# A two-layer decoder trunk: the transposes of two residues' probabilities together, and split weights in six half-tile buffers

## The chip, the cores and the metric

The kernel runs on one core of a Trainium2 chip. The metric is the time of one execution on the device in microseconds (us), lower is better. A core has five engines with a queue each, worked through in order: PE (TensorE, matrix products; its weight loads are shown as PEld), DVE (VectorE), ACT (ScalarE), POOL (GpSimd) and SP (SyncE, which here issues the DMAs). They meet through semaphores.

## What is computed

Two decoder layers over 256 tokens of width 1024, in float32. Layer 0 mixes tokens with three groups of dilated causal window attention, 16 heads each; layer 1 with gated linear attention (GLA). Each is followed by a convolutional gated channel mixer. Cut from the reference:

```python
for i in range(DEPTH):
    mod = jax.nn.silu(c) @ w_ada[i] + b_ada[i]
    sh1, sc1, g1, sh2, sc2, g2 = jnp.split(mod, 6, axis=-1)
    h = rmsnorm(x, norm_mix[i]) * (1.0 + sc1) + sh1
    y = dilated_mixture(h, ...) if i == 0 else gla_mixer(h, ...)
    x = x + g1 * y
    h = rmsnorm(x, norm_ffn[i]) * (1.0 + sc2) + sh2
    x = x + g2 * conv_ffn(h, ...)
return rmsnorm(x, norm_final)
```

In the attention, `p = softmax(q k^T + bias)` over a window, `o = p v` for each of the three groups, and the three outputs are mixed by the softmax of their log sums.

## The kernel before, in words

Activations lie transposed, 8 tiles `x[kt]` of 128 features by 256 tokens. All large products are done three times: an operand is split into a high part in the reduced format `float32r` and the remainder, and `mm3` (L172, matmuls at L175, L176, L177) adds high times high, high times low and low times high.

**Weights.** `split` (L155) loads a tile of up to 2048 columns through SP into one of four `raw` buffers, casts each half on ACT into a `whi` tile (L165), and writes the remainder of each half on DVE into a `wlo` tile (L169). `whi` and `wlo` come from the pool `wspl` (L65), three buffers each of 2048 columns. Matmuls may start on a half as soon as that half is written; a buffer comes free when all matmuls that read any part of its tile are done, and a raw buffer when both subtractions are done. `parts` (L326) hands out columns of the two tiles.

**Stages.** First the norm, while adaLN weights (`ada_chunk`, L129) and the tiles `w0[kt]` (15 blocks of 128 columns: q and k of units 0 and 1, v of unit 0) are loaded. Then eight attention units, `u` = 0 to 7, a pair of heads in all three groups each: products of q, k (`pqk`) and v (`pv`), then `attend` (L408). Then `project` (L569): four tiles `w_out_a[n]`, `n` = 0 to 3, each with columns for kt 0 to 7 in order, 256 each, and `o[kt]` is the output of unit kt. Behind each `n` stand two residuals (L322, tile `py` into `x`), their squares (L199), scaled copies `early_x` (L287) and sums of squares (`sqacc`, L202). `ffn` (L603) then splits the second half of the first `w_up` tile and the second `w_up` tile (the latter held behind `sixth`, the scaled copy of kt 5 and a sum, L605), and `rstd_of` (L184) turns the sums into the norm with two matmuls `ms` (L187). The last residual, kt 7, is held behind the sum before it (L321). Then 22 pairs of up products (`pab`) and the down products (`pd`). Layer 1 has GLA in place of attention, with gates `pr` (`gate`, L887).

**Attention.** In `attend` the queries of a unit are taken as four residues `r` (token index modulo 4), in two halves `h`. For each residue, scores `s` (L419, L426) get their bias and maximum on DVE (L437), exponentials on ACT (L446), and are normed on DVE into `pn` (two instructions, L452 and L453; three `pn` buffers). Three transposes on PE (L457) bring them into a `t` bank, which ACT (even `r`) or DVE (odd `r`) copies to `pt` (L458). The products `po` (L462, L466) follow, and `ohi` on ACT and `olo` on DVE (L471, L472) split the unit's output.

**What sets the order.** The program is written in the order of the source, and a planner in the framework puts each engine's instructions in an order of its own: it simulates the engines, takes at each point what is ready with the earliest place in the source, and gives out a pool's buffers when its model says that one is free. `behind` and `issue_after` hold an instruction behind others in that order. On the chip each engine then keeps to its order, whatever really is ready. So a change of buffers can change the order everywhere.

Of the kernel before, what the change touches and what calls it, by code (L numbers as in the profile page):

```python
# [11 lines left out]
F32 = mybir.dt.float32  # L12
# [6 lines left out]
P = 128  # L19
# [38 lines left out]
def trunk(ctx: ExitStack, tc: tile.TileContext, I, out):  # L58
# [6 lines left out]
    wspl = ctx.enter_context(tc.tile_pool(name="wspl", bufs=3))  # L65
# [17 lines left out]
    c_row = wspl.tile([P, 2048], F32, tag="whi", name="c_row")  # L83
# [12 lines left out]
    oh = wspl.tile([P, 2048], F32, tag="whi", name="oh")  # L96
# [55 lines left out]

    last_load, copied, last_lo = [None], [None], [None]

    def split(src, n, dmas=1, after=((), ()), late=(), low=()):  # L155
        raw = wraw.tile([P, 2048], F32, tag="raw", name="raw")
        for i in range(dmas):
            c = slice(n * i // dmas, n * (i + 1) // dmas)
            last_load[0] = nc.sync.dma_start(raw[:, c], src[:, c])
        hi = wspl.tile([P, 2048], F32R, tag="whi", name="whi")  # L160
        lo = wspl.tile([P, 2048], F32R, tag="wlo", name="wlo")
        for i in range(0, n, n // 2):
            c = slice(i, i + n // 2)
            with behind(*after[i > 0]):
                copied[0] = nc.scalar.copy(hi[:, c], raw[:, c])  # L165
        for i in range(0, n, n // 2):
            c = slice(i, i + n // 2)
            with behind(*(late if i else low)):
                last_lo[0] = nc.vector.tensor_tensor(lo[:, c], raw[:, c], hi[:, c].bitcast(F32), op=ALU.subtract)  # L169
        return hi, lo  # L170
# [155 lines left out]
    def parts(w, at, n=P):  # L326
        return w[0][:, at : at + n], w[1][:, at : at + n]
# [23 lines left out]
    sq = wspl.tile([P, 2048], F32, tag="wlo", name="sq").rearrange("p (k t) -> p k t", k=KT)  # L351
    with behind(last_c):
        keep_warm(4)
    nc.vector.tensor_tensor(sq[:, 0:4, :], x_all[:, 0:4, :], x_all[:, 0:4, :], op=ALU.mult)
    with behind(silu):
        for i in (4, 6):
            last_sq = nc.scalar.activation(sq[:, i : i + 2, :], x_all[:, i : i + 2, :], AF.Square)
    for n in (0, 4):
        for m in (2, 1):
            last_add = nc.vector.tensor_tensor(sq[:, n : n + m, :], sq[:, n : n + m, :], sq[:, n + m : n + 2 * m, :], op=ALU.add)  # L360
# [4 lines left out]
    r = rstd_of([sq[:, 0, :], sq[:, 4, :]])  # L365
# [12 lines left out]
    for kt in range(KT):  # L378
        with behind(*first):
            term = ada_chunk(0, kt, dmas=1 if kt else 2)  # L380
        h.append(normed(0, 0, r, kt))
        if kt:
            w0.append(split(I["w0"][kt], 15 * P))
        else:
            with behind(chain[0][1]):
                w0.append(split(I["w0"][kt], 15 * P, 2, after=((term,), (chain[0][0],))))
# [21 lines left out]
    def attend(u, q, k, v, bias):  # L408
# [32 lines left out]
        for h in range(2):  # L441
            rs = slice(2 * h, 2 * h + 2)
            nc.vector.tensor_scalar(m[:, 4:8][:, rs], m[:, 0:4][:, rs], -1.0, None, op0=ALU.mult)
            for r in (2 * h, 2 * h + 1):
                c = prob[r][:, 0 : KEYS + r]
                nc.scalar.activation(c, c, AF.Exp, bias=m[:, 4 + r : 5 + r], accum_out=m[:, 8 + r : 9 + r])  # L446
            nc.vector.reciprocal(m[:, 12:16][:, rs], m[:, 8:12][:, rs])
            for r in (2 * h, 2 * h + 1):

                f = m[:, 12 + r : 13 + r]  # L450
                pn = att.tile([P, KEYS], F32, tag="pn", name="pn", bufs=3)
                nc.vector.tensor_scalar(grouped(pn[:, 0:T]), by_residue(prob[r][:, 0:T]), f, None, op0=ALU.mult)  # L452
                nc.vector.tensor_scalar(pn[:, T:KEYS], prob[r][:, T + r : KEYS + r], f, None, op0=ALU.mult)  # L453
                t = bank("t", "t")
                for j in range(3):
                    c = slice(P * j, P * j + P)
                    last_t[0] = nc.tensor.transpose(t[:, c], pn[:, c], ident)  # L457
                (nc.vector.tensor_copy if r % 2 else nc.scalar.copy)(pt[:, r, :], t[:, 0:KEYS])  # L458
# [50 lines left out]
    for u in range(NPAIR):  # L509
# [10 lines left out]
        if u == 0:  # L520
# [5 lines left out]
            for kt in range(KT):  # L526
# [3 lines left out]
                wv = parts(w0[kt], 6 * P, NG * P)  # L530
# [3 lines left out]
                for i in range(2 * NG):  # L534
                    mm3(pqk1[i], parts(w0[kt], 9 * P + P * i), h[kt], s and i % 2 == 0, e and i % 2 == 1)
# [67 lines left out]
    def ffn(l, early):  # L603
# [4 lines left out]
        with tc.tile_pool(name=f"ffn{l}", bufs=2) as pool:  # L608
# [57 lines left out]
            for f2 in range(0, KT, 2):  # L666
# [3 lines left out]
                for half, f in ((0, 0), (0, 1), (1, 0), (1, 1)):  # L670
                    w = split(I["w_down"][l, f2 + f, half], 11 * P)
# [300 lines left out]
    y = wspl.tile([P, 2048], F32, tag="whi", name="y")  # L972
    for half in range(2):
        for t, own in enumerate(halves):
            c = slice(512 * half, 512 * half + 512)
            d = y[:, D * t : D * t + D][:, c]
# [29 lines left out]
def _laid_out(a):  # L1006
# [3 lines left out]
    def vec(v):  # L1010
# [76 lines left out]
```

## Time and profile before

| what | value |
|---|---|
| median of three runs | 789.2 us (789.19 to 790.78) |
| profiled execution | 786.27 us, of which its span 784.5 us |
| granted PE clock, mean | 0.996 |
| DVE busy, ACT busy, of the span | 644.3 us, 481.8 us |
| casts L165, subtractions L169 | 274 each, 245.7 and 291.8 us |
| transposes L457 | 96, in groups of three |
| DMA traffic | 184.72 MB, 235 GB/s |

The span goes from the first to the last instruction of the profiled execution; the execution's own time has 1.8 us more around it. In rows of the trace's timeline the first number is the start in us, the second how long the group of instructions took, then engine, line, operation, the tiles (written<-read), shapes and count; brackets at the end hold the idle time of the engine before it and what ended it. In the view of waits a row reads: who waited, for whom, us in total, times, longest.

### The profile page before, as it was taken

What the parts mean: (1) busy time and instruction counts of PE and PEld (TensorE: products, weight loads), DVE (VectorE), ACT (ScalarE), POOL (GpSimd) and SP (SyncE); (2) the same over time, 40 slices, a digit from 0 to 9 for tenths busy, and PEclk for the clock granted to TensorE, in tenths of its full rate; (3) what the DMA queues carried; (4) which work ended last, traced back from release to release, by engine and by line L of the source; (5) the groups of instructions that cost most, each with busy time, mean ns of one, the idle gap of its engine ahead of it and who ended that gap; (6) DMA issues with size and microseconds to landing.
All of it is one profiled execution on the core that took longest, in us unless ns stands there. A gap on an engine that the chain in (4) does not pass through costs nothing.

```text
span 784.5 us, 15887 instructions
## 1 busy us (share of the span) xinstructions
PE 769.3 (98%) x6416; PEld 741.2 (94%) x6416; DVE 644.3 (82%) x1160; ACT 481.8 (61%) x940; POOL 14.3 (2%) x40
## 2 busy tenths in 40 slices
PE   8999999999999998999999999999999999999997
PEld 5999999999999997999999999898999999999997
DVE  6998978878789858999998886797567898899762
ACT  5566555545555657876666555665667866667552
POOL 1000000000000010000000000000010000000000
PEclk9999999999999999999999999999999999999999
DMA  9999577585785726777555985966445765655651
GB/s 347 419 325 343 191 288 264 197 322 195 266 292 200 271 102 227 264 262 267 188 177 201 314 324 183 343 229 229 147 137 190 259 203 178 211 177 210 237 184 54
DMA packets 32616, 184.72 MB, mean 235 GB/s; under 512 B 5852, under 2 KB 7388, under 8 KB 16286
## 3 DMA queue, kind: packets, MB, share of 16 engines
q1 hardware_dynamic: 32160, 183.26, 65.3%
q8 instruction: 50, 0.82, 0.4%
q10 hardware_dynamic: 382, 0.45, 0.2%
q14 instruction: 24, 0.20, 0.1%
HBM read 182.59 MB, written 1.10 MB: 234 GB/s over the span
## 4 chain that ended last, share of the span: by engine, by line
PE 91%; DMA 3%; DVE 3%; ACT 2%; issue 1%; SPq 0%; ACTq 0%; DVEq 0%
PE pab L176 10%; PE pab L175 10%; PE pab L177 10%; PE pqk L175 7%; PE pqk L176 6%; PE pqk L177 6%; PE pd L175 5%; PE pd L177 5%; PE pd L176 5%; PE pv L175 3%; PE pv L176 3%; PE pv L177 3%; PE py L175 2%; PE s L419 2%; PE py L176 2%; PE py L177 1%
## 5 line engine op out<-in xcount | busy, mean ns | idle before, releaser
L169 DVE TENSOR_TENSOR wlo<-raw,whi 128x1024 fp32r<-128x1024 f32 (+3 forms) x274 | 291.8, 1095 | 50.7 <-ACT whi L165 47.9
L165 ACT CAST whi<-raw 128x1024 fp32r<-128x1024 f32 (+3 forms) x274 | 245.7, 944 | 131.5 <-PE pab L176 38.3
L176 PE MATMUL pab<-hlo,whi 128*128 128x256 f32 x672 | 184.8, 276 | 0.0
L177 PE MATMUL pab<-hhi,wlo 128*128 128x256 f32 x672 | 184.8, 276 | 0.0
L175 PE MATMUL pab<-hhi,whi 128*128 128x256 f32 x672 | 183.5, 277 | 0.0
L176 PEld LDWEIGHTS pab<-hlo,whi 128*128 128x128 f32 x672 | 126.1, 188 | 0.2
L177 PEld LDWEIGHTS pab<-hhi,wlo 128*128 128x128 f32 x672 | 126.1, 188 | 0.0
L175 PEld LDWEIGHTS pab<-hhi,whi 128*128 128x128 f32 x672 | 125.3, 188 | 0.1
L175 PE MATMUL pqk<-hhi,whi 128*128 128x256 f32 x440 | 120.7, 286 | 3.6 <-ACT hhi L259 3.0
L176 PE MATMUL pqk<-hlo,whi 128*128 128x256 f32 x440 | 122.0, 281 | 0.0
L138 DVE CUSTOM_DVE_ANT_0 ada_raw<-ada_raw,c_bc 128x1024 f32<-128x1024 f32 x96 | 113.4, 1218 | 10.2 <-DMA ada_raw<-in_w_ada 8.8
L177 PE MATMUL pqk<-hhi,wlo 128*128 128x256 f32 x440 | 121.7, 281 | 0.0
L177 PE MATMUL pd<-ghi,wlo 128*128 128x256 f32 x352 | 97.1, 276 | 0.0
L176 PE MATMUL pd<-glo,whi 128*128 128x256 f32 x352 | 97.1, 276 | 0.0
L175 PE MATMUL pd<-ghi,whi 128*128 128x256 f32 x352 | 96.8, 276 | 0.0
L175 PEld LDWEIGHTS pqk<-hhi,whi 128*128 128x128 f32 x440 | 81.7, 190 | 5.1 <-ACT hhi L259 3.5
L177 PEld LDWEIGHTS pqk<-hhi,wlo 128*128 128x128 f32 x440 | 82.6, 188 | 0.9 <-issue 0.7
L176 PEld LDWEIGHTS pqk<-hlo,whi 128*128 128x128 f32 x440 | 82.8, 188 | 0.4
L177 PEld LDWEIGHTS pd<-ghi,wlo 128*128 128x128 f32 x352 | 66.1, 188 | 0.0
L176 PEld LDWEIGHTS pd<-glo,whi 128*128 128x128 f32 x352 | 66.1, 188 | 0.0
L175 PEld LDWEIGHTS pd<-ghi,whi 128*128 128x128 f32 x352 | 65.9, 188 | 0.0
L648 ACT ACTIVATE r<-pab,small 128x256 f32<-128x256 f32 x86 | 46.5, 559 | 19.2 <-DVE r L651 19.2
(215 smaller groups left out, 1304.5 us busy)
## 6 DMA issues: line engine op xcount, KB each, us to landing
ada_raw<-in_w_ada SPq DMA_DIRECT2D x47, 1024.0 KB, 6.8
raw<-in_w_up SPq DMA_DIRECT2D x42, 1024.0 KB, 4.9
raw<-in_w_down SPq DMA_DIRECT2D x32, 704.0 KB, 5.5
raw<-in_wqk SPq DMA_DIRECT2D x18, 1024.0 KB, 7.4
raw<-in_wv SPq DMA_DIRECT2D x14, 768.0 KB, 4.5
raw<-in_w SPq DMA_DIRECT2D x7, 960.0 KB, 6.8
raw<-in_w_out_a SPq DMA_DIRECT2D x4, 1024.0 KB, 7.2
raw<-in_w_v_b SPq DMA_DIRECT2D x4, 1024.0 KB, 6.1
```

The lines of the kernel that those rows point to most:

```text
L138: nc.vector.tensor_tensor_reduce(w, w, c_bc, op0=ALU.mult, op1=ALU.add, scale=1.0, scalar=0.0, accum_out=dot,)
L165: copied[0] = nc.scalar.copy(hi[:, c], raw[:, c])
L169: last_lo[0] = nc.vector.tensor_tensor(lo[:, c], raw[:, c], hi[:, c].bitcast(F32), op=ALU.subtract)
L175: mm(ps, a[0], b[0], start=start, stop=False)
L176: mm(ps, a[0], b[1], start=False, stop=False)
L177: return mm(ps, a[1], b[0], start=False, stop=stop)
L419: mm(s[:, 0:n], q[0][a][:, r].rearrange("p a b -> p (a b)"), k[0][b][:, 0:n], start=(i == 0), stop=(i == 2))
L648: nc.scalar.activation(r, u[:, :T], AF.Identity, scale=cw[2], bias=col(C_CB + 44 * l + f))
```

## The change

Three things. The pool `wspl` has six buffers of 1024 columns in place of three of 2048, and `split` gives each half of a tile a buffer pair of its own; tiles of at most 1024 columns take one. `cut` says where a tile is cut: in the middle, or at 8 of 15 blocks for `w0` and 6 of 11 for `w_down`, so that no block lies across. The columns of `w0` are laid out anew on the host for the same reason (q and k of unit 1's first group ahead of v). Other users of the pool (`c_row`, `oh`, `sq`, `y`) follow. And in `attend` both `pn` of a half are written ahead of its transposes; the first transpose waits for the second `pn` too, and the second residue's three stand behind the first's.

```diff
-    wspl = ctx.enter_context(tc.tile_pool(name="wspl", bufs=3))
+    wspl = ctx.enter_context(tc.tile_pool(name="wspl", bufs=6))
...
-    def split(src, n, dmas=1, after=((), ()), late=(), low=()):
+    def split(src, n, dmas=1, after=((), ()), late=(), low=(), cut=None):
+        cut = cut or (n // 2 if n > 1024 else n)
         raw = wraw.tile([P, 2048], F32, tag="raw", name="raw")
-        for i in range(dmas):
-            c = slice(n * i // dmas, n * (i + 1) // dmas)
+        for c in (slice(0, cut), slice(cut, n)) if dmas > 1 else (slice(0, n),):
             last_load[0] = nc.sync.dma_start(raw[:, c], src[:, c])
-        hi = wspl.tile([P, 2048], F32R, tag="whi", name="whi")
-        lo = wspl.tile([P, 2048], F32R, tag="wlo", name="wlo")
-        for i in range(0, n, n // 2):
-            c = slice(i, i + n // 2)
-            with behind(*after[i > 0]):
-                copied[0] = nc.scalar.copy(hi[:, c], raw[:, c])
-        for i in range(0, n, n // 2):
-            c = slice(i, i + n // 2)
+        pieces = []
+        for c in (slice(0, cut), slice(cut, n)):
+            if c.stop > c.start:
+                hi = wspl.tile([P, 1024], F32R, tag="whi", name="whi")
+                lo = wspl.tile([P, 1024], F32R, tag="wlo", name="wlo")
+                pieces.append((c.start, c.stop, hi, lo, raw[:, c]))
+        ops = [(hi[:, 0 : b - a], lo[:, 0 : b - a], r) for a, b, hi, lo, r in pieces]
+        if n == 1024:
+            ops = [tuple(z[:, c] for z in ops[0]) for c in (slice(0, 512), slice(512, n))]
+        for i, (hi, lo, r) in enumerate(ops):
+            with behind(*after[i]):
+                copied[0] = nc.scalar.copy(hi, r)
+        for i, (hi, lo, r) in enumerate(ops):
             with behind(*(late if i else low)):
-                last_lo[0] = nc.vector.tensor_tensor(lo[:, c], raw[:, c], hi[:, c].bitcast(F32), op=ALU.subtract)
-        return hi, lo
+                last_lo[0] = nc.vector.tensor_tensor(lo, r, hi.bitcast(F32), op=ALU.subtract)
+        return pieces
...
     def parts(w, at, n=P):
-        return w[0][:, at : at + n], w[1][:, at : at + n]
+        for first, end, hi, lo, _ in w:
+            if first <= at and at + n <= end:
+                return hi[:, at - first : at - first + n], lo[:, at - first : at - first + n]
+        assert False
...
-            w0.append(split(I["w0"][kt], 15 * P))
+            w0.append(split(I["w0"][kt], 15 * P, cut=8 * P))
...
+            pair = []
             for r in (2 * h, 2 * h + 1):
...
-                nc.vector.tensor_scalar(pn[:, T:KEYS], prob[r][:, T + r : KEYS + r], f, None, op0=ALU.mult)
+                last_pn = nc.vector.tensor_scalar(pn[:, T:KEYS], prob[r][:, T + r : KEYS + r], f, None, op0=ALU.mult)
+                pair.append(pn)
+
+            for r, pn in zip((2 * h, 2 * h + 1), pair):
                 t = bank("t", "t")
                 for j in range(3):
                     c = slice(P * j, P * j + P)
-                    last_t[0] = nc.tensor.transpose(t[:, c], pn[:, c], ident)
+                    with behind(*(last_t if r % 2 else ())):
+                        last_t[0] = nc.tensor.transpose(t[:, c], pn[:, c], ident)
+                    if r % 2 == j == 0:
+                        tc.add_manual_dep(last_t[0].ins, last_pn.ins.name,
+                                          mybir.DependencyInfo(mybir.DependencyClass.Sync, mybir.DependencyReason.DATA),
+                                          reason="together")
...
-                wv = parts(w0[kt], 6 * P, NG * P)
+                wv = parts(w0[kt], 8 * P, NG * P)
...
-                    mm3(pqk1[i], parts(w0[kt], 9 * P + P * i), h[kt], s and i % 2 == 0, e and i % 2 == 1)
+                    mm3(pqk1[i], parts(w0[kt], P * (i + (6 if i < 2 else 9))), h[kt], s and i % 2 == 0, e and i % 2 == 1)
...
-                    w = split(I["w_down"][l, f2 + f, half], 11 * P)
+                    w = split(I["w_down"][l, f2 + f, half], 11 * P, cut=6 * P)
...
             qk[:, :, :, :, 0].reshape(KT, P, 6 * P),
+            qk[:, :, 0, :, 1].reshape(KT, P, 2 * P),
             w[:, :, :, 2, 0].reshape(KT, P, 3 * P),
-            qk[:, :, :, :, 1].reshape(KT, P, 6 * P),
+            qk[:, :, 1:, :, 1].reshape(KT, P, 4 * P),
```

More of the change, by code (lines that the diff above doesn't have):

```diff
@@ L80, in exp_ln_after @@
             nc.scalar.preload_act_table_set(EXP_LN)
-    c_row = wspl.tile([P, 2048], F32, tag="whi", name="c_row")
+    c_row = wspl.tile([P, 1024], F32, tag="whi", name="c_row")
     nc.scalar.dma_start(c_row[:1, :D], I["c"])
@@ L95, in trunk @@
     nc.vector.memset(tab[32:33, :], 1.0)
-    oh = wspl.tile([P, 2048], F32, tag="whi", name="oh")
+    oh = wspl.tile([P, 1024], F32, tag="whi", name="oh")
     nc.scalar.dma_start(oh[:33, :NROW], I["onehot"])
@@ L348, in load_bias @@
         return b[:, :]
[L351 removed]
+    sq = [wspl.tile([P, 1024], F32, tag="wlo", name="sq").rearrange("p (k t) -> p k t", k=4) for _ in range(2)]
     with behind(last_c):
         keep_warm(4)
[L354 removed]
+    nc.vector.tensor_tensor(sq[0], x_all[:, 0:4, :], x_all[:, 0:4, :], op=ALU.mult)
     with behind(silu):
         for i in (4, 6):
[L357 removed]
+            last_sq = nc.scalar.activation(sq[1][:, i - 4 : i - 2, :], x_all[:, i : i + 2, :], AF.Square)
     for n in (0, 4):
         for m in (2, 1):
[L360 removed]
+            s = sq[n // 4]
+            last_add = nc.vector.tensor_tensor(s[:, 0:m, :], s[:, 0:m, :], s[:, m : 2 * m, :], op=ALU.add)
         if n == 0:
@@ L382, in trunk @@
         if kt:
-            w0.append(split(I["w0"][kt], 15 * P))
+            w0.append(split(I["w0"][kt], 15 * P, cut=8 * P))
         else:
             with behind(chain[0][1]):
-                w0.append(split(I["w0"][kt], 15 * P, 2, after=((term,), (chain[0][0],))))
+                w0.append(split(I["w0"][kt], 15 * P, 2, cut=8 * P, after=((term,), (chain[0][0],))))
             with behind(copied[0]):
@@ L971, in trunk @@
     nc.scalar.activation(r, ln, AF.Exp, scale=-0.5)
-    y = wspl.tile([P, 2048], F32, tag="whi", name="y")
+    y = [wspl.tile([P, D], F32, tag="whi", name="y") for _ in halves]
     for half in range(2):
```

4 lines of the change are left out of this document (2 added, 2 removed).

## The prediction

> **What bounds the kernel now.** I read the first part of the page for the busy engine, then a table by stage, then what TensorE (PE) itself waited for.
>
> ```profile
> span 784.5 us, 15887 instructions
> ...
> PE 769.3 (98%) x6416; PEld 741.2 (94%) x6416; DVE 644.3 (82%) x1160; ACT 481.8 (61%) x940; POOL 14.3 (2%) x40
> ```
>
> ```profile
> 60.00:285.00 225.00, 224.16 (x1949) 212.35 (x1948) 182.82 (x379) 123.17 (x280) 1.27 (x12) 1.00 0.69 249
> 310.00:470.00 160.00, 160.00 (x1413) 160.00 (x1412) 146.24 (x250) 108.09 (x195) 1.99 (x2) 1.00 0.72 251
> ```
>
> ```profile
> 285.00:310.00 25.00, 22.30 (x172) 20.95 (x171) 20.77 (x39) 19.60 (x45) 2.34 (x2) 1.00 0.49 173
> ```
>
> The columns are the stretch, its length, then the busy time of PE, PE's weight load, VectorE (DVE), ScalarE (ACT) and GpSimd, the granted clock, the DMA share and the rate. PE is full in attention (60 to 285 us) and in the first channel mixer (310 to 470), at a granted clock of 1.00. In the mixer it starts 1413 matmuls in 160 us, one every 0.113 us, without a hole. The poorest later stretch is the seam between the two, 285 to 310, where 2.7 of 25 us are missing. A busy PE hides short stalls, so I add what PE waited for:
>
> ```profile
> PE pqk L175 <- ACT hhi L259: 3.0, 2, 2.4
> PE ms L187 <- DVE sqacc L202: 2.5, 1, 2.5
> ...
> PE pqk L175 <- ACT v L504: 0.6, 1, 0.6
> PE o L855 <- DVE a_t L825: 0.6, 1, 0.6
> PE pr L177 <- DVE wlo L169: 0.5, 1, 0.5
> PE ms L187 <- ACT sq L199: 0.2, 1, 0.2
> PE pv L175 <- DVE k L483: 0.2, 1, 0.2
> ```
>
> The first of them belongs to the start, where PE waits for the second tile of normed activations. The other six, 2.5 + 0.6 + 0.6 + 0.5 + 0.2 + 0.2 = 4.6 us, are what a better order could win behind the start. No change of buffers or order alone makes PE's stream of 6416 matmuls shorter; it can only remove those waits or add new ones. That is my frame: at most 4.6 us to win, and an open side above.
>
> **Where the buffers of split weights bind.** A cast (L165) that waits for a matmul is a cast that waits for a buffer, since matmuls are what reads the buffers. All such waits stand in the view of waits:
>
> ```profile
> ACT whi L165 <- PE pab L176: 38.3, 29, 2.4
> ...
> ACT whi L165 <- PE py L176: 3.9, 2, 2.5
> ...
> ACT whi L165 <- PE pr L176: 2.5, 1, 2.5
> ```
>
> The longest, 38.3 us in 29 waits, lies in the mixers, where PE has no hole at all: ACT is simply as far ahead as three buffers let it be. Smaller pieces let it run half a tile further ahead, and PE gains nothing. In attention the view of L165 alone, 60 to 285 us, names only DMAs as what ended the idle time before casts, most of it this one:
>
> ```profile
>   DMA raw<-in_wv: 29.9, 12
> ```
>
> So no cast of that stretch is seen waiting for a buffer; the raw tile is late, and the raw pool keeps its four buffers. What is left is py (the projection after attention, L586) and pr (the gates of layer 1). The py wait has this surrounding, ACT first, then DVE, then PE:
>
> ```profile
> 284.45 0.37 ACT L471 CAST ohi<-po 128x256 fp32r<-128x256 f32 x1 [4.48 <-PE po L466]
> 286.16 3.04 ACT L165 CAST whi<-raw 128x1024 fp32r<-128x1024 f32 x4 [1.33 <-PE py L176]
> ...
> 293.06 1.98 ACT L165 CAST whi<-raw 128x1024 fp32r<-128x1024 f32 x2
> 294.94 0.72 ACT L199 ACTIVATE sq<-x_all 128x256 f32<-128x256 f32 x2
> ```
>
> ```profile
> 287.81 2.95 DVE L169 TENSOR_TENSOR wlo<-raw,whi 128x1024 fp32r<-128x1024 f32 x3
> 290.68 0.87 DVE L322 SCALAR_TENSOR_TENSOR x_all<-py,mod,x_all 128x256 f32<-128x256 f32 x2
> ...
> 293.72 0.48 DVE L322 SCALAR_TENSOR_TENSOR x_all<-py,mod,x_all 128x256 f32<-128x256 f32 x1 [0.70 <-PE py L177]
> ...
> 296.19 1.22 DVE L169 TENSOR_TENSOR wlo<-raw,whi 128x1024 fp32r<-128x1024 f32 x1
> 297.33 0.42 DVE L202 TENSOR_TENSOR sqacc<-sqacc,sq 128x256 f32<-128x256 f32 x1
> 297.66 0.48 DVE L322 SCALAR_TENSOR_TENSOR x_all<-py,mod,x_all 128x256 f32<-128x256 f32 x1
> ```
>
> ```profile
> 297.80 0.70 PE L187 MATMUL ms<-sqacc,ones_d 128*128 128x256 f32 x2 [2.50 <-DVE sqacc L202]
> 298.70 0.70 PE L187 MATMUL ms<-sq,ones_d 128*128 128x256 f32 x2 [0.20 <-ACT sq L199]
> ```
>
> The four casts at 286.16 are the last piece of w_out_a and the second half of the first w_up tile. Their data had long been there: the last w_out_a load was issued by 264.93 and the first w_up tiles from 269.97 on.
>
> ```profile
> 258.34 6.59 SPq L159 DMA_DIRECT2D raw<-in_w_out_a  x2
> ...
> 269.97 29.68 SPq L159 DMA_DIRECT2D raw<-in_w_up  x5
> ```
>
> ACT stood idle for 4.48 us ahead of 284.45. The casts could not be there, because all three buffers held w_out_a tiles 0, 1 and 2. Each of these is needed for kt 7, the heads of the last unit, which exist only after ohi at 284.45 and olo behind it. So no whole tile comes free before that, though kt 0 to 3, its first half, was multiplied much earlier.
>
> **The change, part by part.** *Six half buffers.* The same bytes, but the first halves of w_out_a tiles 0 and 1 (kt 0 to 3) come free before 284 us, and tile 2's soon too. These are three half buffers, as many as the three pieces need (two of w_out_a tile 3, one of w_up tile 0). Then 3.04 us of casts and, behind them, 2.95 us of subtractions move out of 286 to 291 into idle time ahead of 284. What is late next: the residuals of kt 4 and 5 stood behind those subtractions at 290.68 and come up to 2 us sooner. The two casts of w_up tile 1 at 293.06, held behind scale 5 (the `sixth` of L605), come before 293 instead of standing in front of the squares at 294.94. The subtraction at 296.19, 1.22 us ahead of the last sum on DVE, falls into the gap ahead of 293.72. Then the residual of kt 6, set by PE at 293.72 to 294.20, one square and one sum (0.4 and 0.42 us) let the last residual start near 295.2 instead of 297.66: up to 2.46 us, about the 2.50 + 0.20 = 2.7 us that PE waited. If only ACT's lead counts and that subtraction keeps its place, the gain is about 0.6, half of ACT's 1.33 us of waiting at 286.16, since the squares of kt 4 and 5 still wait for their residuals. I take 2.0, nearer to the full wait, because three things that stood in the chain (casts, subtractions ahead of the residuals, subtraction ahead of the last sum) all hang on the same buffers. SP's loads move with it: raw tiles are released earlier, and the next w_up loads are issued earlier into a stretch whose DMA share is 0.49, so they collide with little.
>
> The other buffer wait, pr 2.5 us, stands beside PE waits of 0.5 and 0.6 us; I count nothing there and keep them for the low end.
>
> *Edges of the pieces.* w0's first piece is 1024 columns instead of 960, the second 896:
>
> ```profile
> L165 ACT CAST whi<-raw 128x1024 fp32r<-128x1024 f32 x158 | 158.0, 1047 | 65.3 <-PE pab L176 32.4 <-DMA raw<-in_wqk 19.6 <-DMA raw<-in_w_v_b 5.2
> ...
> L165 ACT CAST whi<-raw 128x960 fp32r<-128x960 f32 x16 | 15.2, 988 | 3.4 <-DMA raw<-in_w 3.4
> ```
>
> The first cast stands ahead of the first matmul: +0.06 us there, once. The w_down pieces change from 704 and 704 to 768 and 640 and the reordered columns of w0 change no count. Zero.
>
> *Transposes.* Nothing is added but an order: the first transpose of a pair also waits for the second pn, and the second three follow the first. What the order costs on PE:
>
> ```profile
> 179.01 0.49 PE L457 MATMUL t<-ident,pn 128*128 128x128 f32 x3
> ...
> 179.46 0.49 PE L457 MATMUL t<-ident,pn 128*128 128x128 f32 x3
> ```
>
> ```profile
> 88.03 0.88 PE L457 MATMUL t<-ident,pn 128*128 128x128 f32 x6
> ...
> 88.86 0.28 PE L175 MATMUL pqk<-hhi,whi 128*128 128x256 f32 x1
> ```
>
> Three transposes and the matmul behind them take 179.46 - 179.01 = 0.45 us, two such groups 0.90. Six that happen to stand together take, with one matmul, 88.86 - 88.03 = 0.83, and with the other matmul at 0.113 it is 0.94. So standing together gains nothing visible and costs at most 0.04; over 16 pairs 0 to 0.7 us. I take 0, because that one group of six follows a different shape (the 64-row products of po), which the group of three does not. The added wait holds PE, with the projections of the next unit queued behind it, only where PE is early. In ten of the sixteen pairs the second pn was ready at least by the time of the first transpose; in six it was not, from the first of these to the last:
>
> ```profile
> 91.11 0.28 DVE L453 TENSOR_SCALAR pn<-prob,m 128x128 f32<-128x128 f32 x1
> ...
> 91.35 0.49 PE L457 MATMUL t<-ident,pn 128*128 128x128 f32 x3
> ```
>
> ```profile
> 247.85 0.49 PE L457 MATMUL t<-ident,pn 128*128 128x128 f32 x3
> ...
> 248.19 0.29 DVE L453 TENSOR_SCALAR pn<-prob,m 128x128 f32<-128x128 f32 x1
> ```
>
> The lacks are 0.03, 0.05, 0.14, 0.32, 0.45 and 0.63 us, in sum 1.6. The planner knows of the wait and can put matmuls of the next unit in front, of which PE always has some there; I count 0.
>
> *Sum:* -2.0 + 0.06 + 0, about -1.9. The profiled execution took 786.27 us, the span of 784.5 and 1.8 around it; it would come to 784.4. The median of the three runs, 789.2, lies 2.9 above it, and I carry the difference over: **787.3 us**.
>
> **The rivals.** *More goes than the seam* (faster): the planner writes the whole program's order anew, and finer buffers also clear the waits on v, a_t, wlo and k. All six together: 789.2 - 4.6 = 784.6. For it speaks the pr wait for a buffer; against it, that most of these are latencies of a chain and not of a buffer.
>
> *The casts stay* (no change): the planner may leave ACT's order at the seam as it is, or pull the pieces of w_up forward only in part. Then 789.2, less at most 0.6: 788.6 to 789.2. [...]
>
> *The wait for the second pn stops PE* (slower): if transposes keep their places in PE's order, the six lacks above are paid, 1.6 us, with the 0.7 for standing together up to 2.3. It decides where DVE falls behind the plan by more than the matmuls that the plan puts in front, and DVE is busy 182.82 of 225 us there. Without the gain at the seam that is 790.8 to 791.5; with it, 788.9 to 789.6, no change.
>
> **How the numbers follow.** A difference of 0.2%, 1.6 us, is about what a measurement of this kernel can tell from no change. Forecast (gain of 1.6 to 2.7 at the seam, 786.5 to 787.6): 0.40. More than the seam, down to 784.6: 0.12. Casts stay, or gain and loss cancel: 0.26. Transposes stop PE without a gain: 0.22. So faster 0.52, same 0.26, slower 0.22. The range takes in the bounds, 784.6 to 791.5.
>
> **What would show it.** Right: in the seam the casts of w_out_a tile 3 stand ahead of the ohi cast, none waits for py, the last residual starts 2 us earlier after the projection's end, and PE's wait for sqacc falls from 2.5 to under 0.7. The mixers still show 1413 matmuls per 160 us. Wrong: waits of t (L457) on pn appear in PE's list, summing to over 1 us; or casts of the next unit stand on ACT ahead of the exponentials and PE waits for v or k longer than 0.6; or the start moves by more than 0.1 us.

## The result and the profile after

The changed kernel is slower: 795.04 us in the median (791.07 to 796.34, 7 runs), against 789.19 (786.35 to 790.78, 7 runs) for the kernel before on the same chip. The ratio, taken over all runs, is 1.0068, 95% interval 1.0042 to 1.0093 (that of the two medians is 1.0074). The profiled execution took 795.69 us, its span 793.9. A gain of 1.9 us was forecast; the median lies 3.5 us above the upper end of the range, 791.5.

First the same two lines of the page as before, and then the stretches of the table by stage (columns as in the prediction).

```profile
span 793.9 us, 15974 instructions
...
PE 774.1 (98%) x6416; PEld 744.0 (94%) x6416; DVE 646.8 (81%) x1159; ACT 488.2 (61%) x939; POOL 12.1 (2%) x40
```

```profile
285.00:310.00 25.00, 22.52 (x186) 20.71 (x185) 13.32 (x26) 13.10 (x29) 1.49 (x2) 1.00 0.36 120
310.00:470.00 160.00, 160.00 (x1412) 160.00 (x1412) 147.86 (x255) 112.19 (x205) 1.48 (x2) 1.00 0.71 248
520.00:560.00 40.00, 36.79 (x283) 33.99 (x282) 30.84 (x54) 20.33 (x45) 0.62 (x2) 0.96 0.50 180
```

The work is the same, 6416 matmuls, and the channel mixer still starts 1412 of them in 160 us. The last stretch is new: in GLA PE starts 283 matmuls in 40 us, at a mean granted clock of 0.96. Before, the same stretch of time, in which the work stands some 7 us further on, was nearly full:

```profile
520.00:560.00 40.00, 38.90 (x305) 35.76 (x304) 30.89 (x55) 19.22 (x43) 0.62 (x2) 1.00 0.66 241
```

What PE waited for, largest first:

```profile
PE pqk L181 <- ACT hhi L265: 3.5, 1, 3.5
PE kdt L835 <- DVE k_d L827: 2.5, 1, 2.5
PE ms L193 <- DVE sqacc L208: 2.3, 1, 2.3
...
PE t L472 <- DVE pn L464: 1.4, 1, 1.4
...
PE t L472 <- ACT pt L477: 0.6, 1, 0.6
```

The wait for sqacc that was to go is still there, 2.3 in place of 2.5. Others that the prediction's list did not have, k_d in GLA and pn and pt in attention, have come. Where PE as a whole loses time is seen by taking the start of its nth matmul, in us from the span's start (all of these issue 6416, only e14 24 more, in GLA). I worked this table out from the traces; "after" is the changed kernel, "whole" stands for the buffers of before, "half" for those of the change, and the experiments' names are explained below.

```
kernel (buffers)          n=150   n=400   400 to 2300   2300 to mixer 0   GLA
before (whole)            32.54   65.12   218.8         17.8              119.94
e8_before_again (whole)   33.22   65.81   218.2         19.1              119.84
e1_together (whole)       33.58   66.16   219.3         18.9              119.86
e13_before_seam (whole)   32.63   66.54   218.1         16.6              119.86
after (half)              36.57   68.49   222.8         17.4              122.36
e2_halves (half)          35.86   67.78   219.0         18.4              122.04
e3_nowait (half)          36.64   68.56   219.4         18.6              122.12
e12_seam (half)           36.32   68.24   221.5         16.3              121.88
e9_start (half)           31.87   64.79   219.0         20.7              121.94
e14_all (half)            33.45   66.03   218.4         15.8              120.95
```

The first three rows show how far single profiles differ where the kernels' times do not: 1.0 us up to n=400, 1.1 in attention, 1.3 at the seam, 0.1 in GLA. Against them, after loses 2 to 3 us at the start, some 4 in attention, nothing at the seam, and 2.4 in GLA. The loss in GLA is the firm one: every profile with half buffers that has after's order there lies at 121.9 to 122.4. At the start, runs with after's order on all engines scatter (e4 and e10 reach matmul 400 at 66.8, e11 at 69.1), so 2 to 3 us is the size of it and no more.

**The seam, the lines that answer to those of the prediction.** ACT, then DVE, then PE:

```profile
284.98 1.05 ACT L172 CAST whi<-raw 128x1024 fp32r<-128x1024 f32 x1 [0.71 <-PE py L182]
...
291.86 0.37 ACT L490 CAST ohi<-po 128x256 fp32r<-128x256 f32 x1 [0.31 <-PE po L485]
...
301.60 1.98 ACT L172 CAST whi<-raw 128x1024 fp32r<-128x1024 f32 x2
...
303.89 0.40 ACT L205 ACTIVATE sq<-x_all 128x256 f32<-128x256 f32 x1
```

```profile
296.82 1.66 DVE L328 SCALAR_TENSOR_TENSOR x_all<-py,mod,x_all 128x256 f32<-128x256 f32 x4 [2.98 <-PE py L183]
299.43 1.27 DVE L328 SCALAR_TENSOR_TENSOR x_all<-py,mod,x_all 128x256 f32<-128x256 f32 x3 [0.95 <-PE py L183]
...
302.66 1.22 DVE L175 TENSOR_TENSOR wlo<-raw,whi 128x1024 fp32r<-128x1024 f32 x1 [0.45 <-ACT whi L172]
304.32 0.43 DVE L208 TENSOR_TENSOR sqacc<-sqacc,sq 128x256 f32<-128x256 f32 x1 [0.44 <-ACT sq L205]
```

```profile
304.80 0.70 PE L193 MATMUL ms<-sqacc,ones_d 128*128 128x256 f32 x2 [2.28 <-DVE sqacc L208]
```

Before, the first four residuals had come much sooner behind ohi (284.45):

```profile
286.24 1.66 DVE L322 SCALAR_TENSOR_TENSOR x_all<-py,mod,x_all 128x256 f32<-128x256 f32 x4 [0.95 <-PE py L177]
```

The first step came true: the casts of w_out_a tile 3 now stand ahead of ohi (the second of them at 284.98, ohi at 291.86). But the planner spent the early pieces on PE: by the first residual PE has started 151 of the projection's 192 products, where before it had started 123. Tiles 0 to 2 have 144 in all, so products of tile 3 went ahead of their end. DVE waited 2.98 us for the first finished tile, and seven residuals crowd into 296.82 to 300.70. Behind them the two casts of w_up tile 1 (301.60) still stand on ACT in front of the square that the last sum needs (303.89), and a subtraction (302.66) on DVE ahead of that sum. The price of the old place came back at the new one.

**GLA.** DVE ahead of the wait, then PE, then PE's granted clock in stretches of 2 us:

```profile
522.66 1.22 DVE L138 CUSTOM_DVE_ANT_0 ada_raw<-ada_raw,c_bc 128x1024 f32<-128x1024 f32 x1
...
523.80 1.22 DVE L138 CUSTOM_DVE_ANT_0 ada_raw<-ada_raw,c_bc 128x1024 f32<-128x1024 f32 x1
...
524.95 1.75 DVE L769 TENSOR_TENSOR_SCAN cs<-keep,sp 128x768 f32<-128x768 f32 x1
526.62 1.20 DVE L175 TENSOR_TENSOR wlo<-raw,whi 128x1024 fp32r<-128x1024 f32 x1
527.74 0.42 DVE L827 TENSOR_TENSOR k_d<-pqk,e_d 128x256 f32<-128x256 f32 x1
```

```profile
528.21 0.44 PE L835 MATMUL kdt<-ident,k_d 128*128 128x128 f32 x2 [2.49 <-DVE k_d L827]
```

```profile
526.00:528.00 2.00, 0.00 (x0) 1.00 0.93 291
528.00:530.00 2.00, 1.79 (x14) 0.95 0.94 360
530.00:532.00 2.00, 2.00 (x10) 0.50 1.10 426
532.00:534.00 2.00, 2.00 (x10) 0.70 0.88 332
534.00:536.00 2.00, 2.00 (x20) 1.00 0.82 246
```

Two dots of an ada chunk (the rows of L138), a scan over three heads and a subtraction stand in front of a product of 0.42 us for which PE waits 2.5 us. Before, the scan and a subtraction (515.17) stood there too, but the dots came behind:

```profile
513.51 1.75 DVE L750 TENSOR_TENSOR_SCAN cs<-keep,sp 128x768 f32<-128x768 f32 x1
...
516.63 0.42 DVE L808 TENSOR_TENSOR k_d<-pqk,e_d 128x256 f32<-128x256 f32 x1
...
518.16 1.22 DVE L138 CUSTOM_DVE_ANT_0 ada_raw<-ada_raw,c_bc 128x1024 f32<-128x1024 f32 x1
```

After the wait, though PE is full again, the clock is 0.50 and then 0.70 in the mean: 10 matmuls in 2 us, and 20 once it is back at 1.00 from 534 on.

### The profile page after: what moved, and what is told of

Same layout as the page of the kernel before. It is cut to its first block, busy times and chain, and to the rows that moved or that the text cites. A ratio compares the mean times of both kernels' runs of the same rounds, so it can differ in the third digit from the quotient of the medians.

```text
span 793.9 us, 15974 instructions
## 1 busy us (share of the span) xinstructions
PE 774.1 (98%) x6416; PEld 744.0 (94%) x6416; DVE 646.8 (81%) x1159; ACT 488.2 (61%) x939; POOL 12.1 (2%) x40
## 4 chain that ended last, share of the span: by engine, by line
PE 81%; DMA 7%; DVE 6%; ACT 3%; issue 1%; SPq 0%; ACTq 0%; DVEq 0%
PE pab L182 10%; PE pab L181 10%; PE pab L183 10%; PE pqk L181 5%; PE pd L182 5%; PE pd L183 5%; PE pd L181 5%; PE pqk L182 5%; PE pqk L183 5%; DMA raw<-in_wqk 3%; DVE wlo L175 2%; PE pv L181 2%; PE pv L182 2%; PE pv L183 2%; PE py L181 2%; PE py L183 2%
## 5 line engine op out<-in xcount | busy, mean ns | idle before, releaser
L172 ACT CAST whi<-raw 128x1024 fp32r<-128x1024 f32 (+3 forms) x273 | 252.5, 949 | 140.0 <-PE pab L182 53.0
L181 PE MATMUL pqk<-hhi,whi 128*128 128x256 f32 x440 | 122.7, 287 | 4.2 <-ACT hhi L265 3.5
L182 PEld LDWEIGHTS pab<-hlo,whi 128*128 128x128 f32 x672 | 126.1, 188 | 0.2
L183 PEld LDWEIGHTS pab<-hhi,wlo 128*128 128x128 f32 x672 | 126.1, 188 | 0.0
L138 DVE CUSTOM_DVE_ANT_0 ada_raw<-ada_raw,c_bc 128x1024 f32<-128x1024 f32 x96 | 113.5, 1219 | 11.0 <-DMA ada_raw<-in_w_ada 10.9
L182 PE MATMUL pv<-wlo,hhi 128*128 128x384 f32 (+1 forms) x144 | 50.4, 350 | 0.0
```

The lines of the kernel that those rows point to most:

```text
L138: nc.vector.tensor_tensor_reduce(w, w, c_bc, op0=ALU.mult, op1=ALU.add, scale=1.0, scalar=0.0, accum_out=dot,)
L172: copied[0] = nc.scalar.copy(hi, r)
L181: mm(ps, a[0], b[0], start=start, stop=False)
L182: mm(ps, a[0], b[1], start=False, stop=False)
L183: return mm(ps, a[1], b[0], start=False, stop=stop)
```

## The experiments

The theories, by the letters used in what was expected. **A**: the wait for the second pn stops PE. **B**: the planner's new order costs, wherever it happens to change. **C**: a narrower B, that half buffers come free sooner and the planner then puts casts, subtractions and dots in front of a short chain for which PE waits. **D**: the smaller size itself costs. **E**: the start is bound by data and by DVE, with either order. **F**: the clock drops because PE stood idle. **G**: the start's order on DVE and ACT together. All ratios are to the kernel before, on the same chip, with 95% intervals.

**The parts apart.** `e1_together` is the kernel before with the attention hunk alone, `e2_halves` the changed kernel without it.

> The kernel before with the transposes' part of the change alone; the split weights stay in three whole-tile buffers. Theory A (the wait for the second pn stops PE, the rival of the prediction): the changed kernel loses 1.4 + 0.6 us at transposes of one unit and 2.4 us in all on PE's transposes, so this one is slower than before by about 2.4 us, 0.3%, with PE waits for pn or pt of over 1 us in its list. Theory B (every change makes the planner write a new order, and each new order falls on other waits): no wait of PE for pn stands out, and the time goes somewhere else, up or down by 0 to 6 us, with a start and a GLA stage that may differ too.

> The changed kernel with attention's order as before: only the six half-tile buffers (and the columns of w0 that go with them). Theory A: the half buffers cost the rest, 1.8 us at the start and 2.4 us in GLA (PE waits 2.5 us for k_d), so this one is slower than before by some 4 to 5 us, 0.6%, and the PE waits for pn are gone. Theory B: the waits stand at other places than in the changed kernel, the one for k_d may be gone, and the time is anywhere from that of before to that of the changed kernel.

e1 took 788.30 us, ratio 1.0001 (0.9987 to 1.0015); e2 took 792.76, ratio 1.0059 (1.0042 to 1.0076). The transposes together cost nothing by themselves, and A falls as the main cause. The half buffers carry the loss.

**The wait alone.** `e3_nowait` keeps the pairs and the half buffers:

```diff
-                    if r % 2 == j == 0:
-                        tc.add_manual_dep(last_t[0].ins, last_pn.ins.name, ...)
```

> The changed kernel without the wait of the first transpose for the second pn; both pn still stand ahead and the second three transposes still follow the first. Theory A: 2.0 us less than the changed kernel (the 1.4 and 0.6 us of waits in the unit at 250 us go), start and GLA as there. Theory B: the start as there, but other waits in attention and GLA; the difference to the changed kernel may have either sign, up to 5 us.

793.82 us, ratio 1.0069 (1.0051 to 1.0086): no gain that can be told from none. Its profile has no wait for pn, and attention takes 219.4 us in place of 222.8; its seam took 1.2 us more. So by the profiles the wait costs between nothing and some 3 us in the orders that the half buffers brought (e9 has the wait too, and takes 219.0), and nothing in the order of before (e1: 219.3).

**The hold at the seam, taken away.** `e4_nosixth`:

```diff
-        with behind(*sixth):
+        with behind(*(sixth if l else ())):
             w_early.append(split(I["w_up"][l, 1], 2048, late=last_x[1:]))
```

> The changed kernel without the hold of the second w_up tile's casts behind the scaled copy of kt 5, in layer 0. If those casts (1.98 us on ACT) and their first subtraction (1.22 us on DVE) ahead of the last squares and sums are what keeps PE's wait for sqacc at 2.3 us, then they move into the 5.1 us that ACT idles ahead of the residuals, that wait falls below 1 us, and the kernel is 1.5 to 2.3 us faster than the changed one. If the residuals' own chain sets that wait (seven of them crowd into the last 4.7 us of the projection), the wait stays above 1.7 us and the time is that of the changed kernel within 1 us.

793.91 us, ratio 1.0063 (1.0040 to 1.0087). PE waits 2.3 us for sqacc as in after. The casts now stand ahead of the squares, but only at 293.85: ACT idles 4.48 us ahead of them, until a matmul of the projection has ended. Letting those casts go sooner is no cure; the residuals come too late and together.

**Casts held as with whole tiles.** `e5_gla_hold` (in GLA) and `e7_all_hold` (everywhere but at the start, where all eight w0 are split before their matmuls are written down) make each cast wait for the last matmul of the split three tiles earlier; `e6_start_hold` holds only the casts of w0.

```diff
+        earlier = [uses[-4][1]] if hold_on[0] and len(uses) > 3 and uses[-4][1] else []
...
                 copied[0] = nc.scalar.copy(hi, r)
+            for last in earlier:
+                tc.add_manual_dep(copied[0].ins, last.ins.name, ...)
```

```diff
-            w0.append(split(I["w0"][kt], 15 * P, cut=8 * P))
+            w0.append(split(I["w0"][kt], 15 * P, cut=8 * P, after=((chain[kt - 1][0],), ())))
```

> The changed kernel, and in the GLA stage each cast also waits, as with three whole-tile buffers, for the last matmul on the split three before it. Theory C (half buffers come free sooner, so casts go ahead of ACT's and DVE's short chains that PE waits for): casts stand behind the gates' chain again, PE's wait for k_d of 2.3 to 2.5 us goes, the stage from the end of layer 0 to the second up products takes 119.9 us as before and not 122.0 to 122.4, and the kernel is about 2.1 us faster than the changed one: 0.4% over before. Theory D (the GLA loss comes from the tiles' smaller size itself, from more semaphores or smaller pieces, and not from when they come free): the stage stays at 122 us or more, as the waits added here take nothing away.

> The changed kernel, and at the start each w0 cast is held behind the hhi of the tile before it on ACT. Theory C: in the changed kernel the cast of the third w0 tile stands ahead of the second hhi on ACT and waits 2.5 us there for its DMA, so PE's wait for hhi is 3.5 to 4.9 us; with the hold it is 2.4 us or less, and the kernel is 1.2 to 2 us faster than the changed one. Theory E: the start is bound by the DMAs and by DVE, so that wait only moves to a later tile; the time stays within 0.6 us of the changed kernel.

> The changed kernel, and every cast waits for the last matmul on the split three before it, wherever that is written down earlier in the source (not at the start, where all eight w0 splits stand ahead of their matmuls). Theory C: GLA gains 2.1 us and attention and its seam go back to what whole tiles gave, so the time is that of before plus what the start lost: 0.1 to 0.3% over before. Theory D: it stays at 0.6% over before.

> The kernel before, once more, for a second profile: how far do stages of one kernel differ between two executions. The first matmul on w0 came at 12.9 us in the first profile and at 13.7 us in the one with the transposes' part alone, whose start is the same; so I expect 12.9 to 13.8 here, 288.7 us give or take 1.5 from there to the first up products, and 119.9 give or take 0.2 in GLA.

e5 took 796.51 (1.0102, 1.0065 to 1.0139), e6 793.18 (1.0060, 1.0039 to 1.0082), e7 796.19 (1.0096, 1.0062 to 1.0129). `e8_before_again`, the kernel before as it is, took 788.42 in its one run. In e5 and e7 the wait for k_d is gone, as C says, and yet GLA takes 126.1 and 126.3 us: PE stands idle further on, and behind that the clock stays down. The times of both scatter with the clock: e5's six runs go from 792.49 us at a mean clock of 0.995 to 802.03 at 0.983, and the profile is of that slowest one. PE's waits in GLA in e5, and its windows:

```profile
PE o L886 <- ACT ln L205: 1.2, 1, 1.2
...
PE ms L203 <- DVE oacc L898: 0.6, 1, 0.6
```

```profile
562.00:564.00 2.00, 2.00 (x12) 0.50 0.95 373
...
570.00:572.00 2.00, 2.00 (x11) 0.50 0.00 0
572.00:574.00 2.00, 2.00 (x16) 0.96 0.00 0
```

Two holes of 0.60 and 1.22 us, between 558 and 562, are followed by 10 us at half clock. At the start the hold on ACT alone was no cure: in e6 the second tile's products begin at 22.99 in place of 25.11, and yet matmul 150 comes at 35.7 and matmul 400 at 68.4, as in after. That left DVE's order, or the two together.

**GLA's order on DVE.** `e10_gla` keeps the half buffers free and moves only what stood ahead of k_d.

```diff
-            w = split(I["w_qk_b"][hd], 2048)
+            w = split(I["w_qk_b"][hd], 2048, **(dict(after=(e_ds[1:], ()), low=keys) if hd == 2 else {}))
...
         last_key = nc.vector.tensor_tensor(k_t, pk, e_k[:, c], op=ALU.mult)
+        if hd == 0:
+            keys.append(last_key)
+            with behind(last_key):
+                next_ada()
```

> The changed kernel with VectorE's order in the gated stage put right by hand and the half buffers kept: the second gate chunk's dots and the first subtraction of w_qk_b[2] stand behind k_t of the first head, the casts of w_qk_b[2] behind e_d of the other heads. Theory C (half buffers come free sooner, and the planner puts casts, subtractions and dots in front of a short chain for which TensorE waits): the wait of kdt for k_d falls from 2.5 us to under 0.5, no stretch at half clock follows, the gated stage takes 119.9 to 120.4 us in place of 122.4, and the whole about 792 to 793 (ratio to before 1.003 to 1.005). Theory D (the smaller size itself, more instructions or semaphores): the stage stays above 121.5.

794.89 us, ratio 1.0084 (1.0071 to 1.0098): a miss for C as I had put it. The wait for k_d went and the clock stayed at 1.00, but GLA still takes 122.15 us. What PE waits for in this profile there:

```profile
PE ms L193 <- DVE oacc L891: 2.0, 2, 1.4
...
PE pr L183 <- DVE wlo L175: 0.5, 1, 0.5
PE pqk L183 <- DVE wlo L175: 0.4, 1, 0.4
```

These 2.9 us lie further on, at 527 to 558 us; 0.5 of them, for pr, are there in the kernel before as well. DVE has to do the subtractions and dots in this stage somewhere, and in e10's order two dots (543.48) and six subtractions (550.66) stand ahead of the two sums oacc. What the right order would be worth here stays unmeasured; before has it.

**The clock.** `e11_fill` gives PE twelve products that nobody reads, written behind the first head's products, to keep it busy while it would wait for k_d:

```diff
+        if hd == 0:
+            fill = bank("fill", "t")
+            for i in range(12):
+                mm(fill[:, :P], ones_d, ones_d, start=True, stop=True)
```

> The changed kernel with twelve products of a constant by itself put on TensorE behind the last pk product of the first head, about 2.6 us of work that nobody reads, in the place where it waits for k_d. Theory F (the clock drops because TensorE stood idle): granted clock 1.00 in the 6 us behind the place, and the gated stage takes 120.5 to 121.0 us in place of 122.4, although k_d comes no sooner; total 792.5 to 794. Rival (the clock drops for another reason, as DMA traffic of 330 to 430 GB/s at the place): 0.50 to 0.70 stays and the stage stays at 122.0 to 122.6.

792.17 us, ratio 1.0057 (1.0041 to 1.0072). GLA takes 120.96 us, 1.4 less than in after, with some 2.6 us of work in it that nobody reads. The stretches that answer to those of after:

```profile
530.00:532.00 2.00, 2.00 (x17) 1.00 0.79 328
532.00:534.00 2.00, 2.00 (x17) 1.00 1.03 426
```

The DMA rate is of the same size as in after (328 and 426 GB/s, there 426 and 332), and the clock is 1.00. So at this place it is the idle time that makes the clock drop, not the traffic: F holds. The other profiles bear it out. All seven with the hole ahead of kdt, 2.3 to 2.6 us (after, e2, e3, e4, e6, e9, e12), have 3.4 us at 0.50 behind it, and e10, e11 and e14, which do not have it, have none in this stage. The 1.4 us are a less clean measure than was planned: the planner moved the scan and the subtraction on DVE as well, and k_d came at 525.04, 2.7 us sooner than in after though the stage began at the same time, so e11 is not after with the hole filled and nothing else. The size fits, though, since 3.4 us at half clock cost a full PE 1.7.

**The seam's order.** `e12_seam` changes the hold of w_up tile 1 in layer 0; `e13_before_seam` puts the same lines into the kernel before.

```diff
         i = nc.scalar.activation(sq, x[kt], AF.Square)
+        if kt == 6:
+            square_6[0] = i
...
-        with behind(*sixth):
-            w_early.append(split(I["w_up"][l, 1], 2048, late=last_x[1:]))
+        with behind(*(sixth if l else square_6)):
+            w_early.append(split(I["w_up"][l, 1], 2048, late=last_x[1:], low=() if l else last_sum))
```

> The changed kernel with the casts of w_up tile 1 in layer 0 behind the square of residual 6 (ScalarE) and their first subtraction behind the last sum of squares (VectorE). Theory C at the seam: the wait of the norm's sum for sqacc falls from 2.3 us to 0.4 to 0.9, so 1.4 to 1.9 us are won there; total 792 to 793.5. Rival (residuals that all come at the end set it, as the run without the hold suggested): the wait stays above 1.8 and the total at 793.5 to 795.

> The kernel before with the same two holds alone (whole-tile buffers, transposes as before). Theory C at the seam: the wait for sqacc falls from 2.5 us to 0.4 to 1.0 and the total by 1.4 to 2.1 us, to a ratio of 0.9975 to 0.998, which would beat both kernels. Rival (the products behind the norm then wait for w_up tile 1 in place of it): the time moves on, the total within 0.05% of before.

e12 took 791.70 us, ratio 1.0043 (1.0031 to 1.0055), about 2 us less than after. PE's waits at the seam in e12 and in e13:

```profile
PE ms L193 <- ACT sq L205: 1.0, 1, 1.0
...
PE ms L193 <- DVE sqacc L210: 0.4, 1, 0.4
```

```profile
PE ms L187 <- ACT sq L199: 1.4, 1, 1.4
```

e13 took 786.01 us, ratio 0.9968 (0.9956 to 0.9980): faster than both kernels by two held instructions, with the buffers and the transposes of before. The gain that I had looked for at the seam is there. Order alone brings it, not buffers.

**The start's order.** `e9_start`, from the third block of w0 on:

```diff
-        with behind(*first):
+        with behind(*first, *(last_xr if kt > 1 else ())):
             term = ada_chunk(0, kt, dmas=1 if kt else 2)
...
-            w0.append(split(I["w0"][kt], 15 * P, cut=8 * P))
+            before, after = chain[kt - 1]
+            w0.append(split(I["w0"][kt], 15 * P, cut=8 * P, after=((before,), ()), low=(after,)))
```

> The changed kernel with the order at the start put back: from the third block on, the dots of an ada chunk stand behind xr of the tile before (VectorE), the cast of a w0 tile behind hhi and its subtraction behind hlo of the tile before. Theory G (the half buffers' shapes made the planner put a dot of 1.15 us and the casts in front of xr and hhi, and the first product behind the wait starts at 24.2 to 25.1 us in place of 21.2 to 21.6): the start of the second tile's products returns to about 21.5, matmul 400 of TensorE to 65 to 66.5 us (66.8 to 69.1 in the half-buffer kernels so far), and the total falls by 2 to 3 us to 792 to 793. Theory E (data come too late at the start, with either order): matmul 400 stays at 67 to 69 and the total at 794 to 795.

791.76 us, ratio 1.0042 (1.0028 to 1.0056). What stood ahead of the second tile's xr and hhi in after, on DVE and on ACT:

```profile
20.96 1.22 DVE L138 CUSTOM_DVE_ANT_0 ada_raw<-ada_raw,c_bc 128x1024 f32<-128x1024 f32 x1
...
22.11 0.48 DVE L263 SCALAR_TENSOR_TENSOR xr<-x_all,mod,rstd 128x256 f32<-128x256 f32 x1
...
22.57 1.89 ACT L172 CAST whi<-raw 128x1024 fp32r<-128x1024 f32 x2 [2.47 <-DMA raw<-in_w]
...
24.56 0.49 ACT L265 ACTIVATE hhi<-xr,mod 128x256 fp32r<-128x256 f32 x1
```

Before, both came first:

```profile
20.09 0.48 DVE L257 SCALAR_TENSOR_TENSOR xr<-x_all,mod,rstd 128x256 f32<-128x256 f32 x1
20.49 1.22 DVE L138 CUSTOM_DVE_ANT_0 ada_raw<-ada_raw,c_bc 128x1024 f32<-128x1024 f32 x1
...
20.61 0.51 ACT L259 ACTIVATE hhi<-xr,mod 128x256 fp32r<-128x256 f32 x1 [1.32 <-DVE xr L257]
21.74 1.89 ACT L165 CAST whi<-raw 128x960 fp32r<-128x960 f32 x2 [0.62 <-DMA raw<-in_w]
```

So in after xr stood behind a dot, and hhi behind casts that waited 2.47 us for their load. The first products of the second tile, in after and in e9:

```profile
25.11 1.01 PE L181 MATMUL pqk<-hhi,whi 128*128 128x256 f32 x3 [3.53 <-ACT hhi L265]
```

```profile
21.04 0.62 PE L181 MATMUL pqk<-hhi,whi 128*128 128x256 f32 x3 [0.85 <-ACT hhi L266]
```

With the dot, the cast and the subtraction behind xr, hhi and hlo, the products start 4 us sooner (0.7 of them because all of after's start came later) and matmul 400 comes at 64.79, as in before; e14, with the same edit, has 66.03. Both lie under all the runs with after's order, 66.8 to 69.1. G holds, E falls. The loss at the start was in the order on DVE and ACT together (e6 shows that ACT's half of it alone does not help; DVE's alone was not tried); the half buffers stay. In this profile the seam fell badly, with a wait of 3.75 us for sqacc and the clock at half behind it:

```profile
300.00:302.00 2.00, 2.00 (x6) 0.50 0.50 98
```

**All named places at once.** `e14_all` is the changed kernel with the edits of e3, e9, e11 and e12.

> Half buffers kept, with the start's order put back, the two holds at the seam, the twelve constant products at the gated stage, and the pairs without the wait for the second pn. If the named places are the whole loss (start 2 to 3 us, seam 2, clock at the gated stage 1.4, wait for pn about 1), the sum is 795.0 less 6.4 to 7.4 = 787.6 to 788.6, level with before. If a loss stays that no named place explains (theory D, the smaller size itself), the total stays above 790.

786.15 us, ratio 0.9971 (0.9960 to 0.9983), below the lowest that was expected. From 1.0068 to 0.9971 are 0.97%, 7.6 us. One by one the edits had brought 2.0 (start), 2.0 (seam), 0.9 (clock) and nothing measurable (pn), in sum 4.9. Each of these is a difference of two ratios, uncertain by some 2 us to either side, so only the sum is clear of noise; the rest I can't assign, except that attention without the wait took 218.4 us in this profile. D falls as an explanation of the loss: with half buffers and a mended order nothing is lost against before. The comparison that is fair to the seam's gain is the one with e13, which has that gain and whole buffers: 0.9968 there, 0.9971 here, no difference that can be told. So nothing is won by the half buffers either. In GLA alone 1.0 us is still lost (120.95 against 119.9), with the unread products in it.

## Why the prediction was wrong

- *"No change of buffers or order alone makes PE's stream of 6416 matmuls shorter; it can only remove those waits or add new ones."* This frame was right. The failed step is what I then put on its open side: one rival, the pn wait, and no term at all for new orders outside the seam. From *"no cast of that stretch is seen waiting for a buffer"* in attention, and *"I count nothing there"* for the buffer wait of pr in GLA, I went on as if nothing changed there. The runs showed new orders in place of that nothing: dots and casts ahead of xr and hhi at the start, 2 to 3 us (e9), and in GLA dots ahead of k_d or, where these are moved (e10), waits further on, 2.2 to 2.4 us with or without half clock. The half buffers alone cost 0.59%, some 4.6 us (e2).
- *"I take 2.0"* at the seam is the other step that failed. The casts moved as foreseen. That the residuals keep their places and only lose what stands in front of them was wrong: PE's order changed as well, and the first residual came 5 us behind ohi (296.82) where it had come 1.8 behind it (286.24). Measured: 2.28 us of wait in place of 2.50. The 2 us exist, and two holds take them without any buffer (e13, 2.5 us; e12, 2.0).
- *w0's edges, "+0.06"*, priced a longer cast. The order around that cast changed, and with it 2 to 3 us. "The start moves by more than 0.1 us" stood among the signs of a wrong prediction, and it did.
- *Transposes, 0*: right by themselves (e1: 1.0001). The rival "the wait for the second pn stops PE" came true in the changed kernel in one place, unit 6, by a plan that the half buffers had altered. Its two pairs were among the six that I had counted; at the first PE stood 1.39 us, of which 0.55 lie between the first pn and the second, and at the second the 0.65 us were for pt. The other four places have no wait.
- *"The casts stay"*: they did move, but that hardly anything was to be had from the buffers, as this rival's 788.6 to 789.2 had it, is what e14 beside e13 shows.
- *Mixers, 0*: right, 177.3 us each before and after.
- Not in the sum at all: a PE hole can cost more than its length. In after's GLA 3.4 us at half clock follow the hole of 2.49 us, which is up to 1.7 us more.
- The list of PE's waits behind the start has one more row than the 4.6 us count, 0.2 us at the last norm; it changes nothing.

## What to carry to other kernels

When a planner orders the program, finer buffers are a change of order everywhere: look, in every stage where a short chain feeds a full PE (norm, gates, first tile), at what may now be put in front of its links on the same queue. Where one wait at one place is the aim, hold the instructions that stand in front of that chain: two holds gave 0.9968 here, and six half buffers gave 1.0068. In these runs a hole of 2.3 to 3.75 us on PE cost its length and, where the clock fell behind it, half of each 3.4 us at 0.50 besides: 1.7 us in after's GLA. In e5 that half was some 5 us, behind holes of 0.60 and 1.22 us.

## What the hardware showed

The seven holes ahead of kdt, 2.3 to 2.6 us, and those of the seam in e8 (2.5 us) and e9 (3.75) were followed by a granted clock of 0.50, and the time at half clock came in pieces of one length. In after's GLA the windows above give 0.05, 0.50 and 0.30 of 2 us each lost to the clock, so 3.4 us at 0.50. The other k_d holes give 3.4 us too, e9's seam 6.8, e5 10.2: once, twice and three times 3.41 us. It does not always follow: the kernel before had a hole of 2.50 us at the seam and 0.20 soon after with the clock at 1.00, and the same kernel's other profile (e8) has this behind it:

```profile
298.00:300.00 2.00, 2.00 (x5) 0.55 0.04 16
```

The length of the hole alone does not tell whether the clock falls: in after it stayed at 1.00 behind the seam's hole of 2.28 us and fell behind the 2.49 us in GLA, and before and e8 differ with 2.5 us each. What decides it, the runs here do not show. The clock records of before and after hold no value but 0.50 and 1.00, and their first piece at 0.50, at the start, has the same 3.41 us (from 20.65 us in before, from 24.62 in after). Open too is e5 (and e7, the same): three pieces at 0.50, with PE full all the while, behind holes of 0.60 and 1.22 us.

One row more was a surprise: the dots of L138, 1.2 us a piece on DVE, are twice in this study (start and GLA) part of what stood between PE and its next operand.
